# Weight blocks split into two parts by transfers instead of by engines, in a three-layer transformer kernel

## The chip, the cores and the metric

The kernel runs on one core of one Trainium2 chip. The metric is the device time of one execution in microseconds (us). The engines that appear below are PE (TensorE, matrix products; PEld is its weight load), DVE (VectorE), ACT (ScalarE), POOL (GpSimd) and SP (SyncE, which here does nothing but issue transfers). Each has its own queue and works through it in order.

## The reference, cut to what matters

The model has three layers on 512 tokens of 1024 features, all in float32: a mixer (forgetting attention and chunked attention) and a squared-relu MLP, a second mixer (stick-breaking and latent attention) and a second such MLP, and a third, hybrid mixer with a SwiGLU. Almost all of its time goes into products with weight matrices:

```python
x = x + even_mixer(h, w_in_ab, ..., w_out_ab)
x = x + jnp.square(jax.nn.relu(rmsnorm(x, g) @ w_up)) @ w_down
x = x + odd_mixer(h, positions, w_in_cd, ..., w_out_cd)
...
h = h + (jax.nn.silu(u @ w_gate) * (u @ w_up)) @ w_down
```

## The kernel before, in words

Float32 products are made from two short numbers. Every operand is kept as a rounded part (hi, type float32r) and the rest (lo), and a product W x is summed from three matmuls: hi hi, hi lo and lo hi. Activations are split where they arise. Weights are split where they are loaded.

The weights lie in DRAM as one flat array of blocks of 128 partitions by at most 1120 columns; most are 128x1024, 512 KB, which is eight stationary pieces of 128x128. `wblock` (line 584) brings one block: it loads the block into a raw tile (tag `wr`) with a transfer on SP's queue, ACT copies the raw tile into `wh`, which rounds it, and DVE subtracts `wh` from the raw tile into `wl`. There are two buffers of each of the three tags (`BUFS`, line 543). `gemm` (line 594), `gemm_iter` and `gemm_tok` call `wblock` and issue 24 matmuls of 512 columns to a full block: per piece two with `wh` and one with `wl`. In the last down projection some blocks go to tiles of tag `h`.

The order of the instructions is made on the host. The program is first recorded (`Recorder.add`, line 286), with the tiles that each instruction reads and writes. `Recorder.schedule` (line 390) then runs a list schedule: it keeps a clock for each engine, takes the ready instruction of lowest priority number, and hands out a tag's buffers in a fixed turn. The order that comes out for each engine is the order of its queue on the chip. Its costs are in `cost` (line 321) and `LAT` (line 355): a transfer takes 450 ns of its issuing engine when the source is DRAM, then 650 ns, then its bytes at 360 per ns, one transfer after the other; what waits for it starts 910 to 950 ns later if SP issued it, and 70 to 135 ns later if POOL issued it. In the kernel before, POOL issues no transfer at all. POOL's queue holds sums of squares (`acc`), the product of the SwiGLU's gate with a norm row (`T<-T,rbc`), softmax scaling, masks and the small `rsqrt` of the norms.

The program's stretches in time: first mixer 0 to 262 us, first MLP to 618, second mixer to 922, second MLP to 1278, third mixer to 1718 (its last 118 us are output projections with no attention beside them), SwiGLU and final norm to the end. Nearly every instruction carries line 371 in the profile, since one line issues all that was recorded; so the rows are told apart by the names of the tiles.

Of the kernel before, what the change touches and what calls it, by code (L numbers as in the profile page):

```python
# [11 lines left out]
F32 = mybir.dt.float32  # L12
# [6 lines left out]
T = 512  # L19
# [16 lines left out]
# --------------------------------------------------------------------------  # L36
# host side: layouts only
# --------------------------------------------------------------------------
class Packer:
    """Weights as one flat array of contiguous [128, width] blocks."""  # L40
# [12 lines left out]
    def stationary(self, key, w, cols=None):  # L53
        """[128 K, 128 M] pieces in the order (m, kt), eight to a block."""
        if cols is not None:
            w = w[:, cols]
        k, m = w.shape
        kt, nm = k // 128, m // 128
        sub = w.reshape(kt, 128, nm, 128).transpose(2, 0, 1, 3).reshape(nm * kt, 128, 128)
        blocks = [  # L60
            np.ascontiguousarray(sub[s:s + 8].transpose(1, 0, 2)).reshape(128, -1)
            for s in range(0, nm * kt, 8)
        ]
        self._add(key, blocks, (kt, nm))

    def moving(self, key, w, cols=None):
        """[128 K, N] pieces, as many k tiles to a block as WB columns hold."""
        if cols is not None:
            w = w[:, cols]
        k, n = w.shape  # L70
        kt = k // 128
        sub = w.reshape(kt, 128, n)
        blocks = [
            np.ascontiguousarray(sub[s:s + WB // n].transpose(1, 0, 2)).reshape(128, -1)
            for s in range(0, kt, WB // n)
        ]
        self._add(key, blocks, (kt, n))
# [8 lines left out]
class Columns:  # L86
    """Small [128, n] arrays side by side."""
# [137 lines left out]
# --------------------------------------------------------------------------  # L225
# order of the instructions: what the program does is recorded first, then
# issued engine by engine in the order of a list schedule
# --------------------------------------------------------------------------
# [20 lines left out]
class Recorder:  # L249
# [13 lines left out]
    @contextmanager  # L263
    def later(self, k):
        """what is recorded inside yields to the next k instructions, but for those that wait for it"""
        old, self.shift = self.shift, k
        yield
        self.shift = old

    def flush(self):  # L270
        """all that is recorded so far comes first"""
        for op in self.ops:
            op.prio = min(op.prio, len(self.ops))
# [80 lines left out]
    # from the end of one instruction to the start of a dependent one on another engine  # L354
# [26 lines left out]
    def sequence(self):  # L381
        """the instructions by priority: each before those that wait for it, what comes later in its own order"""
        first = math.inf
        for op in reversed(self.ops):
            op.prio = min([op.prio] + [self.ops[k].prio for k in op.succ])
            if op.group:
                op.prio = first = min(op.prio, first)
        return sorted(self.ops, key=lambda o: (o.prio, o.n))
# [110 lines left out]
# --------------------------------------------------------------------------  # L499
# chip side  # L500
# --------------------------------------------------------------------------
class Net:
# [21 lines left out]
    def fetch(self, m, tag="x"):  # L524
        """residual tile m on chip"""
        if self.x[m] is None:
            self.x[m] = self.tl(tag, [128, 512])
            self.nc.sync.dma_start(self.x[m], self.xd[m])
        return self.x[m]
# [13 lines left out]
    BUFS = {"x": 8, "T": 3, "G": 3, "P": 3, "wr": 2, "wh": 2, "wl": 2, "V": 8, "o": 6, "KK": 4, "QS": 2, "AB": 2, "h": 8, "X4": 4,  # L543
# [29 lines left out]
    def split(self, dst, src, scale=None):  # L573
        """dst[:, 0] + dst[:, 1] = src (* scale per partition), two short parts."""
        nc = self.nc
        hi, lo = dst[:, 0], dst[:, 1]
        if scale is None:
            nc.scalar.activation(hi, src, AF.Copy)
            nc.vector.tensor_tensor(lo, src, hi.bitcast(F32), ALU.subtract)
        else:  # L580
            nc.scalar.activation(hi, src, AF.Copy, scale=scale)
            nc.vector.scalar_tensor_tensor(lo, src, scale, hi.bitcast(F32), ALU.mult, ALU.subtract)

    def wblock(self, key, b, tags=("wh", "wl")):
        nc = self.nc
        off, w = self.pk.index[key][0][b]
        raw = self.tl("wr", [128, WB])[:, :w]
        hi, lo = (self.tl(t, [128, WB if t[0] == "w" else 1024], F32R) for t in tags)
        nc.sync.dma_start(raw, self.ins["w"][off:off + 128 * w].rearrange("(p c) -> p c", p=128))
        nc.scalar.activation(hi[:, :w], raw, AF.Copy)  # L590
        nc.vector.tensor_tensor(lo[:, :w], raw, hi[:, :w].bitcast(F32), ALU.subtract)
        return hi, lo

    def gemm(self, key, mov, evac, tags="gggggggg", cols=slice(0, 512), kept=None):
        """out[m] = W[:, m]^T mov; evac(m, psum)."""
# [17 lines left out]
    def gemm_tok(self, key, stat, evac, blk=None):  # L613
        """out[token tile i] = stat^T W; evac(i, psum)."""
# [33 lines left out]
    def mean_cols(self, acc, n, eps=None):  # L648
        """[128 tokens, tiles] mean of squares (+ eps)."""
        nc = self.nc  # L650
        ps = self.psum("s")
        nt = acc.shape[1] // 128
        for i in range(nt):
            nc.tensor.matmul(ps[:, i:i + 1], acc[:, 128 * i:128 * i + 128], self.c("ones"), start=True, stop=True)
        ms = self.small(nt)
        if eps is None:
            nc.vector.tensor_scalar(ms, ps[:, :nt], 1.0 / n, None, ALU.mult)
        else:
            nc.vector.tensor_scalar(ms, ps[:, :nt], 1.0 / n, eps, ALU.mult, ALU.add)
        return ms  # L660
# [8 lines left out]
    def rows(self, col, outs):  # L669
        """[128, 512] with col[token] in every row; outs = [(tag, factor)]."""  # L670
# [12 lines left out]
    def prep(self, m, gain, spill=False, sq=0):  # L683
        """operand x*g of feature tile m and its share of the sum of squares."""
# [29 lines left out]
    def to_stack(self, ab):  # L714
        """per head [hi; lo]"""
# [8 lines left out]
    def to_dup(self, ab):  # L724
        """per head a tile (hi, lo) with its rows twice"""
# [18 lines left out]
    def softmax(self, i, passes, bias, gate=None):  # L744
        """P [128 q, keys] from negated scores, normalised."""
# [14 lines left out]
    def turn(self, ps_list):  # L760
        """four P tiles -> per key tile j [128 keys, (hi, lo), q]"""
# [19 lines left out]
    def fold(self, o, dst, u):  # L781
        """O = rows 0:64 + rows 64:128, into half u of dst"""
# [5 lines left out]
    def v_tiles(self, key, stat, rcol, extra=None, blk=None):  # L788
        """value tiles [128 tokens, 4 heads, (hi, lo), 64]"""
# [55 lines left out]
    def out_part(self, key, ops):  # L845
        """first part of an output projection, one residual tile at a time"""
# [14 lines left out]
    def even_mixer(self):  # L861
# [20 lines left out]
        # sums within a token tile, and of the tiles one, two and three before  # L882
# [196 lines left out]
    def sincos(self, pos, freq, tag="strip"):  # L1079
        """cos and sin of position * frequency (frequencies along partitions)"""  # L1080
# [10 lines left out]
        # n = nh + nl, both short enough for exact products with the parts of 2 pi  # L1091
# [24 lines left out]
    def rope(self, pa, pb, c, s, tag):  # L1116
        """(x1 c - x2 s, x2 c + x1 s), each split"""
# [56 lines left out]
    def prep2(self, m):  # L1174
        """x * final gain * mixer gain, sums of x^2 and of (x * final gain)^2"""
# [13 lines left out]
    def hybrid_mixer(self):  # L1189
# [19 lines left out]
        # for the residual of the second block  # L1209
        rx, = self.rows(r1, [("strip", 1.0)])  # L1210

        # lambda
# [13 lines left out]
        # differential attention  # L1226
# [30 lines left out]
        # keys, values and gates of the second branch  # L1257
# [71 lines left out]
        # gated output of the first branch  # L1329
# [86 lines left out]
    def gemm_iter(self, key, mov):  # L1416
        """like gemm, one output tile at a time"""
# [76 lines left out]
    def compress(self, n, src):  # L1494
        """silu(windows @ w1), hidden units along partitions: [128, 2, (group, 32 windows)]"""
# [34 lines left out]
    def cmp_tiles(self, hk, hv, late):  # L1530
# [5 lines left out]
        # values: the windows of a group four times along the partitions  # L1536
# [12 lines left out]
        # keys: [hi; hi], [lo; lo] over (group, window)  # L1549
# [3 lines left out]
        # the windows of a group between zeros, so that a slice puts them at any of four places  # L1553
# [213 lines left out]
```

## Time and profile before

| | |
|---|---|
| time, median of 3 runs | 2093.58 us (2093.03 to 2095.36) |
| span of the profiled execution | 2093.9 us |
| PE busy | 2038.8 us, 97% |
| DVE, ACT, POOL busy | 1131.0, 896.5, 399.1 us |
| transfers on SP's queue | 230.25 MB, 35.9% of 16 DMA engines |

The page names busy time by engine, the busy share in slices, the transfer queues, the chain of work that ended last, and the costliest groups of instructions. A group's name is output<-inputs by tile names. Idle time before an instruction is put down to what released it. Times are us unless marked ns.

### The profile page before, as it was taken

Reading aid. Unit: us, or ns where it says so; the run is one execution under the profiler, and the core shown is the slowest. Engines: PE = TensorE matmul, PEld = TensorE weight load, DVE = VectorE, ACT = ScalarE, POOL = GpSimd, SP = SyncE. Lnnn points to the kernel's source line nnn. Section 1 sums busy time; section 2 is a strip of 40 time slices with the busy share of each in tenths; the row PEclk is TensorE's granted clock in tenths of the full one; section 3 lists DMA queues with packets and bytes.
Section 4 is the critical chain, followed back from the end, with each engine's and each line's share of the span. In section 5 each row is a group of like instructions: output and inputs, shape, how many; then the busy total and the mean of one; then the engine's idle time right before and its main releaser. Section 6 shows DMA issues by size and latency. Waiting matters only on the chain. (4 is left out here: it accounts for less than half of the span.)

```text
span 2093.9 us, 27228 instructions
## 1 busy us (share of the span) xinstructions
PE 2038.8 (97%) x9958; PEld 1688.3 (81%) x9958; DVE 1131.0 (54%) x2033; ACT 896.5 (43%) x1621; POOL 399.1 (19%) x524
## 2 busy tenths in 40 slices
PE   8999999999999999899999999989999999999998
PEld 7887878888888877778888888877788888888887
DVE  5657853443445666774434344766786644333334
ACT  5556542322335555643323243544685542222224
POOL 2343210000022453220000014212240221011013
PEclk9999999999999999999999999999999999999999
DMA  6445623323244415632333234474113222223222
GB/s 197 133 129 157 186 91 92 100 91 101 91 142 122 111 58 129 181 104 91 100 92 98 94 120 131 126 185 126 57 41 111 92 100 91 101 91 101 90 101 81
DMA packets 80294, 232.00 MB, mean 111 GB/s; under 512 B 11424, under 2 KB 15392, under 8 KB 80160
## 3 DMA queue, kind: packets, MB, share of 16 engines
q1 hardware_dynamic: 80160, 230.25, 35.9%
q8 instruction: 79, 1.29, 0.3%
q14 instruction: 55, 0.45, 0.1%
HBM read 183.04 MB, written 10.49 MB: 92 GB/s over the span
## 5 line engine op out<-in xcount | busy, mean ns | idle before, releaser
L371 PE MATMUL psg<-h,wh 128*128 128x512 f32 x2688 | 855.4, 396 | 0.9 <-ACT h L371 0.6
L371 ACT ACTIVATE wh<-wr 128x1024 fp32r<-128x1024 f32 (+3 forms) x313 | 326.6, 1043 | 864.3 <-PE psg L371 687.4
L371 PEld LDWEIGHTS psg<-h,wh 128*128 128x128 f32 x2688 | 504.3, 189 | 108.2 <-ACT h L371 1.4
L371 PE MATMUL psg<-h,wl 128*128 128x512 f32 x1344 | 532.5, 396 | 1.0 <-DVE wl L371 0.7
L371 DVE TENSOR_TENSOR wl<-wr,wh 128x1024 fp32r<-128x1024 f32 (+3 forms) x313 | 385.0, 1230 | 58.8 <-ACT wh L371 54.8
L371 PEld LDWEIGHTS psg<-h,wl 128*128 128x128 f32 x1344 | 253.9, 189 | 56.6 <-DVE wl L371 2.7
L371 PE MATMUL psg<-KK,wh 128*128 128x512 f32 (+1 forms) x788 | 240.6, 387 | 0.4 <-DVE V L371 0.2
L371 DVE TENSOR_TENSOR x<-psg,x 128x512 f32<-128x512 f32 (+1 forms) x120 | 78.2, 654 | 290.8 <-PE psg L371 290.7
L371 POOL TENSOR_TENSOR acc<-acc,T 128x512 f32<-128x512 f32 (+1 forms) x50 | 73.5, 1471 | 789.6 <-issue 639.5
L371 PE MATMUL psg<-V,wh 128*128 128x512 f32 (+1 forms) x672 | 207.9, 390 | 1.0 <-DVE G L371 1.0
L371 PEld LDWEIGHTS psg<-KK,wh 128*128 128x128 f32 x788 | 146.6, 188 | 32.2 <-ACT o L371 0.5
L371 PE MATMUL psg<-KK,wl 128*128 128x512 f32 (+1 forms) x394 | 151.7, 385 | 0.0
L371 PEld LDWEIGHTS psg<-V,wh 128*128 128x128 f32 x672 | 126.2, 189 | 29.0 <-ACT wh L371 1.1
L371 DVE SCALAR_TENSOR_TENSOR T<-psg,rbc 128x512 f32<-128x512 f32 x64 | 44.3, 692 | 174.9 <-PE psg L371 172.6
L371 PE MATMUL psg<-V,wl 128*128 128x512 f32 (+1 forms) x336 | 131.6, 392 | 0.0
L371 ACT ACTIVATE x<-x,sm 128x128 f32<-128x128 f32 (+1 forms) x192 | 106.6, 558 | 52.5 <-DVE sm L371 52.0
L371 PE MATMUL psg<-o,wh 128*128 128x512 f32 x384 | 127.7, 401 | 0.8 <-ACT wh L371 0.5
L371 PE MATMUL psg<-wh,h 128*128 128x256 f32 (+2 forms) x560 | 114.2, 291 | 6.7 <-ACT wh L371 6.7
L371 PE MATMUL pso<-pt,V 128*128 128x128 f32 (+3 forms) x432 | 108.0, 337 | 3.5 <-ACT pt L371 1.9
L371 POOL TENSOR_SCALAR x<-x,sm 128x128 f32<-128x128 f32 (+1 forms) x112 | 66.5, 599 | 173.2 <-DVE sm L371 121.0
L371 PEld LDWEIGHTS psg<-wh,h 128*128 128x128 f32 x560 | 92.0, 193 | 8.4 <-ACT wh L371 6.7
L371 POOL TENSOR_TENSOR T<-T,rbc 128x512 f32<-128x512 f32 x22 | 39.3, 1785 | 285.3 <-ACT T L371 285.3
(263 smaller groups left out, 2673.8 us busy)
## 6 DMA issues: line engine op xcount, KB each, us to landing
wr<-in_w_dram SPq DMA_DIRECT2D x302, 512.0 KB, 3.5
KK<-AB SPq DMA_DIRECT2D x48, 256.0 KB, 5.4
QS<-AB SPq DMA_DIRECT2D x48, 128.0 KB, 3.9
x<-xs SPq DMA_DIRECT2D x24, 256.0 KB, 3.3
xs<-P SPq DMA_DIRECT2D x16, 256.0 KB, 3.8
xs<-x SPq DMA_DIRECT2D x16, 256.0 KB, 2.0
h<-AB SPq DMA_DIRECT2D x16, 256.0 KB, 3.8
KK<-AB SPq DMA_DIRECT2D x32, 128.0 KB, 2.4
```

Source lines behind the costliest of these rows:

```text
L371: op.inst = getattr(getattr(nc, op.eng), op.name)(*op.args, **op.kw)
```

## The change

`wblock` no longer has a raw tile. A transfer issued by POOL (`nc.gpsimd.dma_start`) reads the float32 block from DRAM and casts it into the float32r tile `wh`. ACT writes the negated `wh` into `wl`. A second transfer issued by POOL reads the same block from DRAM again and adds it onto `wl` (`accum_op=ALU.add`), which leaves block minus `wh`. DVE's subtraction is gone. `wh` and `wl` have three buffers each instead of two; tag `wr` is no longer used. The diff also takes out comments and docstrings, which is left out here.

```diff
-    BUFS = {"x": 8, "T": 3, "G": 3, "P": 3, "wr": 2, "wh": 2, "wl": 2, "V": 8, ...
+    BUFS = {"x": 8, "T": 3, "G": 3, "P": 3, "wr": 2, "wh": 3, "wl": 3, "V": 8, ...
...
     def wblock(self, key, b, tags=("wh", "wl")):
         nc = self.nc
         off, w = self.pk.index[key][0][b]
-        raw = self.tl("wr", [128, WB])[:, :w]
         hi, lo = (self.tl(t, [128, WB if t[0] == "w" else 1024], F32R) for t in tags)
-        nc.sync.dma_start(raw, self.ins["w"][off:off + 128 * w].rearrange("(p c) -> p c", p=128))
-        nc.scalar.activation(hi[:, :w], raw, AF.Copy)
-        nc.vector.tensor_tensor(lo[:, :w], raw, hi[:, :w].bitcast(F32), ALU.subtract)
+        src = self.ins["w"][off:off + 128 * w].rearrange("(p c) -> p c", p=128)
+        nc.gpsimd.dma_start(hi[:, :w], src)
+        nc.scalar.activation(lo[:, :w], hi[:, :w].bitcast(F32), AF.Copy, scale=-1.0)
+        nc.gpsimd.dma_start(lo[:, :w], src, accum_op=ALU.add)
         return hi, lo
```

## Rows read from the trace of the kernel before

**Rows 1.** The page, part 1: busy us, share of the span, instructions.
```profile
span 2093.9 us, 27228 instructions
PE 2038.8 (97%) x9958; PEld 1688.3 (81%) x9958; DVE 1131.0 (54%) x2033; ACT 896.5 (43%) x1621; POOL 399.1 (19%) x524
```
**Rows 2.** Busy by stretch: us, engines busy (x), PEclk, DMA share, GB/s.
```profile
0.00:262.00 262.00, 250.13 (x1428) 214.18 (x1429) 178.59 (x413) 148.05 (x323) 87.82 (x157) 1.00 0.55 160
262.00:618.00 356.00, 353.88 (x1531) 288.90 (x1530) 154.68 (x176) 118.28 (x150) 14.24 (x9) 0.99 0.31 99
618.00:922.00 304.00, 284.12 (x1525) 238.04 (x1524) 207.10 (x401) 169.62 (x362) 110.78 (x184) 0.99 0.43 122
1278.00:1718.00 440.00, 429.06 (x2208) 351.64 (x2208) 292.41 (x691) 230.84 (x489) 109.64 (x120) 0.99 0.35 106
```
**Rows 3.** Instructions on tile wr by stretch: us, DVE busy (x), ACT busy (x).
```profile
262.00:618.00 356.00, 77.73 (x64) 67.95 (x64) 0.99 0.31 99
1600.00:1718.00 118.00, 27.91 (x22) 23.30 (x22) 1.00 0.27 95
```
**Rows 4.** The chain that ended last, in order of time: start us, us, what.
```profile
1721.74 345.57 PE psg L371 x1582
```
**Rows 5.** Timeline of ACT in the SwiGLU: start us, us, instruction, [idle before <-releaser].
```profile
1754.52 1.06 ACT L371 ACTIVATE wh<-wr 128x1024 fp32r<-128x1024 f32 x1 [3.97 <-PE psg L371]
1755.48 0.61 ACT L371 ACTIVATE T<-T 128x512 f32<-128x512 f32 x1
...
1765.56 1.06 ACT L371 ACTIVATE wh<-wr 128x1024 fp32r<-128x1024 f32 x1 [3.97 <-PE psg L371]
```
**Rows 6.** Waits, whole kernel: engine, for what: us in total, times, longest us.
```profile
ACT wh L371 <- PE psg L371: 687.4, 204, 5.2
...
PE psg L371 <- ACT wh L371: 7.2, 2, 6.7
...
PE psg L371 <- DVE wl L371: 2.0, 4, 1.0
...
SPq L371 <- DVE wl L371: 1347.4, 270, 27.4
```
**Rows 7.** Costliest groups: the subtraction: xcount | busy us, mean ns | idle before.
```profile
L371 DVE TENSOR_TENSOR wl<-wr,wh 128x1024 fp32r<-128x1024 f32 (+3 forms) x313 | 385.0, 1230 | 58.8 <-ACT wh L371 54.8
```
**Rows 8.** Tile wr, 1722 to 2045: ns min/median/max, first and last start; landing us.
```profile
L371 SPq DMA_DIRECT2D wr<-in_w_dram x59: 327/328/328, 1723.3 to 2044.1; - x59
L371 ACT ACTIVATE wh<-wr x58: 1061/1064/1067, 1726.8 to 2041.7; 128x1024 fp32r<-128x1024 f32 x58
...
  ACT wh L371: 10.1, 40
...
DMA to landing us min/median/max: 3.1/3.2/3.8
```
**Rows 9.** Busy in that stretch, with DMA share and GB/s.
```profile
1722.00:2045.00 323.00, 323.00 (x1405) 264.04 (x1405) 125.58 (x139) 86.86 (x103) 39.07 (x22) 1.00 0.28 95
```
**Rows 10.** POOL by group: xcount | busy us, mean ns | idle before.
```profile
L371 POOL TENSOR_TENSOR T<-T,rbc 128x512 f32<-128x512 f32 x22 | 39.3, 1785 | 285.3 <-ACT T L371 285.3
...
L371 POOL TENSOR_TENSOR sm<-sm,cst 128x4 f32<-128x4 f32 (+1 forms) x15 | 14.7, 979 | 59.0 <-DVE sm L371 59.0
```
**Rows 11.** Tile wr, whole kernel: the issues and the landing.
```profile
L371 SPq DMA_DIRECT2D wr<-in_w_dram x317: 327/328/2131, 1.7 to 2056.1; - x159
...
DMA to landing us min/median/max: 2.0/3.5/8.4
```
**Rows 12.** Busy before and after the second MLP's norm.
```profile
915.00:920.00 5.00, 4.00 (x17) 2.74 (x15) 4.43 (x6) 4.87 (x7) 2.82 (x3) 1.00 0.39 108
920.00:925.00 5.00, 4.28 (x15) 3.70 (x16) 1.23 (x2) 2.56 (x4) 1.69 (x2) 0.62 0.29 101
```
**Rows 13.** Timeline of PE there.
```profile
918.50 0.50 PE L371 MATMUL psg<-h,wh 128*128 128x512 f32 x1
920.72 1.45 PE L371 MATMUL pss<-cst,acc 128*128 128x1 f32 x8 [1.72 <-POOL acc L371]
922.03 0.77 PE L371 MATMUL psg<-h,wh 128*128 128x512 f32 x1
```

More of the change, by code (lines that the diff above doesn't have):

```diff
@@ L541, in c @@
         return self.ct[:, o:o + n]
-    BUFS = {"x": 8, "T": 3, "G": 3, "P": 3, "wr": 2, "wh": 2, "wl": 2, "V": 8, "o": 6, "KK": 4, "QS": 2, "AB": 2, "h": 8, "X4": 4,
+    BUFS = {"x": 8, "T": 3, "G": 3, "P": 3, "wr": 2, "wh": 3, "wl": 3, "V": 8, "o": 6, "KK": 4, "QS": 2, "AB": 2, "h": 8, "X4": 4,
             "sm": 16, "sm32": 3, "rbc": 1, "rbcq": 1, "strip": 2}
```

## The prediction

> **What bounds the kernel now.** I read the busy times first, then stretches, then one block in the steady part, then who waits for weights. PE is busy 2038.8 us of a span of 2093.9 us, so 55 us is all that is not PE [rows 1]. In the first MLP it is busy 353.88 of 356 us [rows 2], and the chain that ended last is one unbroken run of 1582 matmuls, 345.57 us, in the SwiGLU [rows 4]. There a block comes round every 5.5 us: the ACT copies of the rows shown lie 1765.56 - 1754.52 = 11.04 us apart with one between them [rows 5], and 59 block loads were issued in 320.8 us, 320.8/58 = 5.53 us [rows 8]. That is PE's own pace for 24 matmuls. The reader is to see in the waits that the weights come early: ACT waits 687.4 us in all for PE to free a `wh` buffer, while PE waits 7.2 us for `wh` and 2.0 us for `wl`; SP's queue waits 1347.4 us to be allowed to load the next raw block [rows 6]. So the work of splitting is hidden today, and what the change takes away from DVE is worth almost nothing by itself. What it puts in its place must stay under 5.53 us a block.
>
> **Blocks at full pace and others.** The first MLP has 64 blocks [rows 3]; the other MLP stretches show the same 64 each, and the output projections at the end of the third mixer 22 [rows 3]. That is 214 blocks at 5.53 us. Of 317 loads [rows 11] 103 remain, in mixer stretches of 262 + 304 + (440 - 118) = 888 us, 8.6 us apart. POOL is busy 87.82 + 110.78 + 109.64 = 308 us in the three mixers [rows 2], about 2.4 us a block for their 126 blocks.
>
> **Removed.** 313 subtractions, 385.0 us of DVE [rows 7]. They lie beside PE; DVE is at 54% [rows 1]. Worth 0 to the 2.0 us that PE waits for `wl` [rows 6]. SP loses 317 issues of 0.33 us [rows 11] and its 1347 us of waiting for raw buffers, so that the operand moves queued behind them go out sooner. PE's gaps bound that gain at 55 us in all; I take 5 us. ACT's pass stays, one per block at 1.06 us [rows 8], now after the transfer instead of before PE's release: no difference in busy time.
>
> **Added: two POOL issues per block.** POOL issued no transfer, so no row shows the price. Ends: 0.33 us, SP's issue of the same transfer [rows 8], and 1.79 us, POOL's costliest group [rows 10]. I take 0.98 us, its 128x4 operation [rows 10]: a POOL instruction with almost no data, which is nearest to one that only prepares a transfer. 634 of them are 621 us on top of 399 [rows 1], so POOL is not full; order is what matters.
>
> **Added: the casting transfer.** It moves the bytes of today's load. Ends 3.1 us from issue to landing, the least in the SwiGLU [rows 8], and 8.4 us, the most anywhere [rows 11]. I take the median 3.2 us of the undisturbed stretch [rows 8]. On the engines a block takes 0.28 x 5.53 = 1.55 us [rows 9].
>
> **Added: the accumulating transfer.** It reads the block from DRAM again and must also read what lies in `wl`. Ends: 1.55 us of the DMA engines, if the addition costs nothing, and 8.4 us by the slowest landing [rows 11]. I take two loads' worth, 3.1 us, because twice the bytes are read. The Trainium skill, page "Collectives: The Full Stack", section "The bandwidth ceiling: the fold count and why AG ≠ RS ≠ AR", says that a summing transfer needs two source reads on one ring and that copying is 1.93 times as fast; no run here shows that. As an estimate from that page the transfer would be 1.55 x 1.93 = 3.0 us and the total below about 25 us lower.
>
> **Added: a wait in POOL's queue.** The accumulating issue waits for ACT, which waits for the cast's landing. Queued behind it on POOL are the next block's cast and whatever sums, masks and softmax scalings the plan put there; PE and DVE wait for those, and ACT's evacuations queue behind the negation. The plan's own figures put the accumulating issue 0.45 + 0.65 + 1.46 + 0.075 + 0.95 + 0.17 = 3.75 us after the cast's issue (costs in the code), and the next cast when PE frees a buffer, one block later. So POOL's order is cast, accumulate, cast, accumulate, and one round of it is a chain: cast lands 3.2, hand-off to ACT and back 2 x 0.25 (10.1 us of waits over 40 copies [rows 8]) with ACT 1.06 between, accumulate issued. If the next cast is queued right behind it, its data come after the accumulating transfer's on the same DMA engines. The issue time drops out, because transfers move while the next is prepared: round = 3.2 + 0.5 + 1.06 + accumulating transfer = 4.76 + 3.1 = 7.9 us. With an addition that costs nothing it is 4.76 + 1.55 = 6.3 us; with nothing in front of the cast and SP's price of issue 4.76 + 0.33 = 5.1 us, under PE's 5.53.
>
> **The sum.** At 7.9 us the 214 full-pace blocks cost 214 x (7.9 - 5.53) = 507 us. In the mixers a round of 7.9 us fits into 8.6 us if POOL's other 2.4 us fall into the waits, and overruns by 1.7 us if they don't; I take half, 103 x 0.85 = 88 us. Minus 5 us. The third buffer does not help against a round that repeats for every block; it covers latency only: two blocks' time, 11.06 us, from release to need. Total 2094 + 507 + 88 - 5 = 2684 us, against the profiled span of 2093.9 us, which is the median of the runs to 0.02%. I say **2680 us**. With the ends of the terms: additions that cost nothing 2094 + 214 x 0.77 + 0 - 5 = 2254 us; a cast that lands only after 8.4 us, round 13.1 us, 2094 + 214 x 7.53 + 103 x 4.5 - 5 = 4164 us.
>
> **The rivals.** *Nothing to see* (0.10): casts find free buffers early and run ahead, round 5.1 us, PE stays the bound: 2085 to 2120 us. For it: 4.76 us leaves 0.8 us of slack. Against: the plan lets a cast go only when PE has released a buffer, and the accumulating transfer is due half a microsecond before. *Faster* (0.06): the same, and three buffers with SP's queue emptied close PE's gaps in the mixers, where 55 us lie less the start and the final norm; it decides below a round of 5.53 us, and gives 2075 us. *Half hidden* (0.17): addition at the price of a copy, round 6.0 to 6.5: 2190 to 2300 us. *PE loses its clock* (0.22): each late block leaves PE idle. At the second MLP's norm PE stood still for 1.72 us, had only eight one-column matmuls, and the granted clock went from 1.00 to 0.62 [rows 12, 13], that is, from 2.4 GHz to mostly 1.2 GHz; a 512-column matmul then took 0.77 us in place of 0.50 [rows 13]. At half the clock a block takes up to 2 x 5.53 = 11.1 us: 2094 + 214 x 5.53 + 103 x 2.5 = 3535 us. It decides where the idle time per block is near that gap; at 7.9 us it is 2.4 us, and matmuls of full width stand on both sides, so I give it the smaller chance. The Trainium skill, page "TensorE: Matmul & The Clock Gate", section "What's actually happening", holds the low clock to be the default that only activity lifts; by that rule, too, a starved PE is slowed twice; the rows agree. *The change does something else*: if the cast kept all bits, `wl` would be zero, with the same transfers and time; that moves no number here.
>
> **How the numbers follow.** Forecast (round 6.5 to 9 us, 2300 to 3000 us) 0.45; nothing to see 0.10; faster 0.06; half hidden 0.17; lost clock or transfers slower than I took 0.22. A measurement of this kernel can tell about 0.2% from no change, 4 us. Faster by more than that: 0.06 and 0.01 of nothing to see, 0.07. Within it 0.05. Slower 0.88. The range leaves out faster and part of nothing to see below, and the far part of the last case above: 2110 to 3550 us.
>
> **What would show it.** Right: in the MLPs POOL's accumulating issue waits for ACT, ACT's negation waits for the landing of the cast, and PE waits for the transfer into `wl`, over 2 us a block; the blocks come every 7 to 9 us; the DMA share rises above 0.5. Wrong in size: the pace of the blocks, from which the two landing times can be read apart. Wrong in kind: PE still 97% busy, or PE waiting in the mixers only, or the granted clock well below 1.

## The result and the profile after

The changed kernel takes 2839.94 us (2837.65 to 2851.07, median of 4 runs) against 2094.47 us (2093.03 to 2100.32) of the kernel before beside it. The ratio is 1.357, with a 95% interval of 1.354 to 1.360: slower by 745 us. The forecast was 2680 us, slower, in a range of 2110 to 3550 us. The profiled execution has a span of 2837.5 us, 743.6 us more than that of before.

Busy time first, to be held against [rows 1]: engine, us, share of the span, instructions.

```profile
span 2837.5 us, 27499 instructions
PE 2296.1 (81%) x9958; PEld 1809.7 (64%) x9958; DVE 769.2 (27%) x1716; ACT 896.5 (32%) x1621; POOL 805.7 (28%) x1158
```

PE fell from 97% to 81%, and no other engine took its place: DVE lost its 362 us net, POOL gained 407 us for 634 transfers and is still idle for 72% of the span. Where no engine is busy all the time, a chain of waits is the likely limit. To see where, the span is cut at the norms' `rsqrt` on POOL, which lie in both kernels at the start of an MLP and at its end. Before (the stretches with an MLP or the SwiGLU, then the mixers), then after; us, busy us of PE, PEld, DVE, ACT and POOL (instructions), granted clock, share of the DMA engines, GB/s.

```profile
272.15:628.11 355.96, 355.95 (x1563) 291.68 (x1562) 149.99 (x170) 118.45 (x150) 13.61 (x8) 0.99 0.32 101
922.45:1279.26 356.81, 356.62 (x1544) 291.11 (x1544) 150.72 (x175) 121.67 (x155) 21.77 (x16) 0.99 0.32 101
1719.61:2093.90 374.29, 364.14 (x1727) 303.71 (x1725) 147.32 (x178) 108.05 (x144) 55.73 (x41) 0.99 0.27 93
```
```profile
0.00:272.15 272.15, 258.16 (x1460) 220.41 (x1461) 188.56 (x424) 151.60 (x329) 92.04 (x159) 0.99 0.55 158
628.11:922.45 294.34, 274.47 (x1462) 229.48 (x1461) 201.97 (x395) 165.91 (x355) 107.18 (x182) 0.99 0.43 120
1279.26:1719.61 440.35, 429.50 (x2210) 351.92 (x2211) 292.41 (x691) 230.84 (x489) 108.77 (x119) 0.99 0.35 106
```

```profile
0.00:334.62 334.62, 277.73 (x1458) 231.85 (x1459) 149.17 (x390) 157.74 (x333) 132.35 (x229) 0.93 0.76 180
334.62:864.70 530.08, 415.81 (x1562) 316.61 (x1560) 72.60 (x106) 114.43 (x146) 101.49 (x137) 0.91 0.58 131
864.70:1228.51 363.81, 300.85 (x1464) 247.13 (x1464) 165.71 (x359) 166.70 (x355) 151.05 (x256) 0.90 0.63 141
1228.51:1754.86 526.35, 416.83 (x1559) 318.27 (x1560) 74.61 (x112) 121.02 (x155) 110.08 (x144) 0.91 0.59 133
1754.86:2298.56 543.70, 466.75 (x2199) 368.78 (x2198) 236.29 (x636) 230.22 (x489) 176.46 (x228) 0.93 0.60 138
2298.56:2837.50 538.94, 418.17 (x1719) 327.06 (x1719) 70.86 (x114) 106.40 (x143) 134.30 (x168) 0.91 0.56 128
```

The three stretches with an MLP or the SwiGLU grew by 530.1 - 356.0, 526.4 - 356.8 and 538.9 - 374.3 us, 508 us in all. The mixers were 272.2, 294.3 and 440.4 us; they grew by 62.5, 69.5 and 103.3 us, 235 us in all. Together that is the 743.6 us. A block of the first MLP (64 of them) takes 530.1/64 = 8.28 us in place of 356.0/64 = 5.56 us.

The waits of the whole kernel after, against [rows 6]: engine, for what: us in total, times, longest.

```profile
POOL wl L371 <- ACT wl L371: 1529.5, 273, 13.0
ACT wl L371 <- DMA wh<-in_w_dram: 1202.8, 223, 12.8
...
PEld psg L371 <- DMA wl<-in_w_dram: 498.9, 220, 6.3
PE psg L371 <- DMA wl<-in_w_dram: 407.0, 212, 5.9
...
POOL wh L371 <- PE psg L371: 137.6, 64, 9.8
```

POOL waits for ACT, ACT for the cast's landing, PE for the accumulating transfer. POOL waits 137.6 us for PE to free a buffer, where ACT waited 687.4 us for that before: over the whole kernel, free buffers are not what is short. One round in the SwiGLU, from the timelines of POOL, then ACT, then PE (start us, us, instruction, [idle before <-releaser]):

```profile
2443.33 0.85 POOL L371 DMA_DIRECT2D wl<-in_w_dram  x1 [6.51 <-ACT wl L371]
2443.88 0.87 POOL L371 DMA_DIRECT2D wh<-in_w_dram  x1
2451.42 0.85 POOL L371 DMA_DIRECT2D wl<-in_w_dram  x1 [6.67 <-ACT wl L371]
```
```profile
2450.06 1.06 ACT L371 ACTIVATE wl<-wh 128x1024 fp32r<-128x1024 f32 x1 [7.03 <-DMA wh<-in_w_dram]
```
```profile
2440.63 0.50 PE L371 MATMUL psg<-KK,wl 128*128 128x512 f32 x1 [2.05 <-DMA wl<-in_w_dram]
...
2448.80 0.50 PE L371 MATMUL psg<-KK,wl 128*128 128x512 f32 x1 [2.35 <-DMA wl<-in_w_dram]
```

The cast is issued 0.55 us after the accumulating transfer of the block before; ACT starts 6.18 us later, runs 1.06 us, and 0.30 us on the next accumulating transfer goes out: 0.55 + 6.18 + 1.06 + 0.30 = 8.09 us, and PE gets its block every 8.17 us. The landings in the first MLP, 380 to 840 us (first `wh`, then `wl`; min, median, max us from issue):

```profile
DMA to landing us min/median/max: 5.9/6.2/6.8
```
```profile
DMA to landing us min/median/max: 5.2/5.5/5.8
```

The cast, a transfer of 512 KB like the one that took 3.2 us in [rows 8], lands after 6.2 us: it was queued right behind the accumulating one, and the experiments below show what that costs.

### The profile page after: what moved, and what is told of

Read it like the earlier page. It is cut to its first block, busy times and chain, and to the rows that moved or that the text cites. A ratio compares the mean times of both kernels' runs of the same rounds, so it can differ in the third digit from the quotient of the medians.

```text
span 2837.5 us, 27499 instructions
## 1 busy us (share of the span) xinstructions
PE 2296.1 (81%) x9958; PEld 1809.7 (64%) x9958; DVE 769.2 (27%) x1716; ACT 896.5 (32%) x1621; POOL 805.7 (28%) x1158
## 4 chain that ended last, share of the span: by engine, by line
issue 55%; PE 16%; POOL 16%; DMA 9%; ACT 2%; DVE 1%; SPq 0%; POOLq 0%; DVEq 0%; ACTq 0%
PE psg L371 9%; POOL wh L371 6%; POOL wl L371 5%; DMA wh<-in_w_dram 4%; DMA wl<-in_w_dram 3%; PE pss L371 3%; PE psp L371 2%; PE pso L371 2%; POOL T L371 1%; POOL acc L371 1%; ACT wl L371 1%; POOL x L371 1%; DMA x<-in_x_dram 1%; POOL G L371 0%; DVE x L371 0%
## 5 line engine op out<-in xcount | busy, mean ns | idle before, releaser
L371 PE MATMUL psg<-h,wh 128*128 128x512 f32 x2688 | 917.6, 421 | 0.0
L371 ACT ACTIVATE wl<-wh 128x1024 fp32r<-128x1024 f32 (+3 forms) x313 | 325.4, 1040 | 1564.8 <-DMA wh<-in_w_dram 1202.8
L371 PE MATMUL psg<-h,wl 128*128 128x512 f32 x1344 | 580.1, 432 | 198.2 <-DMA wl<-in_w_dram 198.1
L371 POOL DMA_DIRECT2D wl<-in_w_dram x313 | 272.6, 873 | 1637.9 <-ACT wl L371 1529.5
L371 PEld LDWEIGHTS psg<-h,wh 128*128 128x128 f32 x2688 | 545.9, 204 | 122.2 <-issue 2.3
L371 POOL DMA_DIRECT2D wh<-in_w_dram x313 | 244.8, 782 | 149.4 <-PE psg L371 137.6
L371 PE MATMUL psg<-KK,wh 128*128 128x512 f32 (+1 forms) x788 | 279.9, 441 | 1.2 <-DVE G L371 0.7
L371 PEld LDWEIGHTS psg<-KK,wl 128*128 128x128 f32 x394 | 87.7, 223 | 219.9 <-DMA wl<-in_w_dram 203.1
L371 PE MATMUL psp<-cst,x 128*128 128x128 f32 x440 | 89.7, 289 | 21.8 <-POOL x L371 13.8
L371 PE MATMUL psg<-o,wl 128*128 128x512 f32 x192 | 82.8, 435 | 28.2 <-DMA wl<-in_w_dram 28.2
```

Source lines behind the costliest of these rows:

```text
L371: op.inst = getattr(getattr(nc, op.eng), op.name)(*op.args, **op.kw)
```

## The experiments

The first five test the theory that the round is a chain of cast, negation and addition whose transfers share one queue. What is compared in each is the length of the first MLP, 64 blocks, from norm to norm; the kernel before, run beside them, took 2095.8 to 2098.6 us. Each time of an experiment is one run.

**The addition's price.** The second transfer casts the block over `wl` instead of adding to it.

```diff
-        nc.gpsimd.dma_start(lo[:, :w], src, accum_op=ALU.add)
+        nc.gpsimd.dma_start(lo[:, :w], src)
```

> The second transfer overwrites wl with a cast of the block instead of adding onto it, so wl holds the wrong numbers; order, waits and buffers stay as in the changed kernel. Theory (a round of POOL's queue sets the pace: the cast's data stand behind the accumulating transfer's on the DMA engines, then landing, ACT, next issue): only the accumulating transfer's 3.1 us shrinks to 1.55 us, the round from 8.1 to about 6.5 us, 2094 + 214 x 0.95 + some 50 us in the mixers = about 2350 us. Rival (the transfers' fixed latency and POOL's issue set the pace, not the bytes that the addition reads): 8.1 us a block stay, 2800 to 2840 us.

Measured: 2415.7 us; the first MLP 419.5 us, 6.55 us a block. Its stretch, and the landings of `wh` and of `wl` in it:

```profile
316.79:736.31 419.52, 374.04 (x1561) 287.15 (x1559) 72.61 (x106) 114.77 (x146) 78.25 (x136) 1.00 0.52 166
```
```profile
DMA to landing us min/median/max: 4.4/4.6/5.0
```
```profile
DMA to landing us min/median/max: 3.7/3.8/4.3
```

Without the addition the second transfer lands 1.7 us sooner (3.8 against 5.5), the cast queued behind it 1.6 us sooner (4.6 against 6.2), and the round is 1.73 us shorter. So the addition alone costs 424 us of the 745. The rest is there with two casts. The pace is the expected one, the total 66 us above it.

**No second transfer.** `wl` stays the negated `wh`.

```diff
-        nc.gpsimd.dma_start(lo[:, :w], src, accum_op=ALU.add)
```

> The second transfer is left out: wl stays the negated wh, which is wrong for lo; the cast on POOL's queue and ACT's negation stay. Theory (the chain through POOL's queue needs the second issue): nothing on POOL waits for ACT any more, casts go as soon as PE releases a buffer, three buffers cover 3.2 + 0.9 + 1.3 us; PE is the bound again, 2085 to 2110 us. Rival (a cast issued by POOL is slow by itself, or POOL's queue delays it behind softmax work): the mixers stay 100 to 235 us longer, 2200 to 2350 us.

Measured: 2160.4 us, between the two expectations. In the first MLP a block takes 360.0/64 = 5.62 us and PE is busy throughout:

```profile
295.26:655.21 359.95, 359.95 (x1573) 293.66 (x1573) 72.75 (x106) 118.92 (x146) 44.27 (x73) 1.00 0.35 100
```

One cast per block is hidden there; its landing is 3.8 us. What is left of the 65 us lies mostly in the mixers (295.3, 304.4 and 460.0 us: 23 + 10 + 20 us more than before). The three kernels give the engines' time of each transfer in the same stretch, DMA share times pace: 0.35 x 5.62 = 1.97 us a block with the cast alone, 0.52 x 6.55 = 3.41 with a second cast behind it, 0.58 x 8.28 = 4.80 with the accumulating one. By these shares a second cast adds 1.44 us, an accumulating transfer 2.83 us, 1.97 times as much. Each of the two without the other, over the whole kernel (this run, and the addition alone further below; q0 is the queue of POOL's transfers: packets, MB, share of the 16 engines' span), gives a smaller factor:

```profile
q0 software_dynamic: 45648, 162.81, 26.5%
```
```profile
q0 software_dynamic: 45648, 162.81, 36.2%
```

That is 0.265 x 2158.7 = 572 us for the casts and 0.362 x 2626.1 = 951 us for the same bytes added, 1.66 times as much. The Trainium skill ("Collectives: The Full Stack", "The bandwidth ceiling: the fold count and why AG ≠ RS ≠ AR") has copying 1.93 times as fast as summing, measured between the ranks of a ring; the 1.66 to 1.97 of these runs lie around that.

**Two buffers.** The third buffer of each tag is undone, the rest is the changed kernel.

```diff
-    ... "wr": 2, "wh": 3, "wl": 3, ...
+    ... "wr": 2, "wh": 2, "wl": 2, ...
```

> The third buffers of wh and wl are undone, all else as in the changed kernel. Theory (the round in POOL's queue sets the pace, and buffers don't): with two buffers a block is ready 0.2 + 4.1 + 1.3 + 5.4 = 11 us after PE released the one two before, so two blocks take 11 + 5.5 us, 8.2 us each, the same pace by another limit; 2840 to 2950 us. Rival (the latency of the whole way from release to wl is the limit already with three buffers, about 8.1 x 3 - 5.5 = 19 us): two buffers give (19 + 5.5)/2 = 12 us a block, about 3900 us.

Measured: 3201.2 us, 595.0/64 = 9.30 us a block, between the two. From POOL's timeline:

```profile
599.31 0.87 POOL L371 DMA_DIRECT2D wl<-in_w_dram  x1 [6.70 <-ACT wl L371]
603.64 0.55 POOL L371 DMA_DIRECT2D wh<-in_w_dram  x1 [3.46 <-PE psg L371]
610.21 0.86 POOL L371 DMA_DIRECT2D wl<-in_w_dram  x1 [6.01 <-issue]
610.76 0.87 POOL L371 DMA_DIRECT2D wh<-in_w_dram  x1
```

Every other cast now waits for PE, too. So the third buffer is worth 1.0 us a block, 361 us of the whole: it does hide latency, and the forecast that it "does not help against a round that repeats" holds only for the part of the round that is left.

Because the casts wait for PE here, they follow the accumulating transfer at different distances, and this shows whether the time between the two issues matters. In the SwiGLU, POOL, and the landing of the cast of 2714.42:

```profile
2712.23 0.89 POOL L371 DMA_DIRECT2D wl<-in_w_dram  x1 [2.10 <-ACT wl L371]
2714.42 0.56 POOL L371 DMA_DIRECT2D wh<-in_w_dram  x1 [1.30 <-PE psg L371]
```
```profile
DMA to landing us min/median/max: 4.5/4.5/4.5
```

Issued 2.19 us after the accumulating transfer, this cast lands 2.19 + 4.5 = 6.7 us after that one's issue. Over the whole run the median of this time is 6.9, 7.0, 6.9 and 6.7 us for casts issued 0.5 to 1, 1 to 1.5, 1.5 to 2 and 2 to 2.5 us behind (41, 38, 37 and 11 of them). In the changed kernel, where the distance is 0.55 us, it is 0.55 + 6.2 = 6.75 us. Within 2.5 us a cast that is issued later does not land later: its landing is set by the accumulating transfer ahead of it and not by its own issue.

**The order in POOL's queue.** Nothing is changed but the order: where a cast follows an accumulating transfer in POOL's queue, it is put in front of it, so that the cast travels while ACT's result is awaited.

```diff
-            for op in (self.schedule() if reorder else ops):
+            order = self.schedule() if reorder else ops
...
+                if add(order[a]) and order[b].name == "dma_start" and not add(order[b]):
+                    after[b] = order[a]
...
+            for op in order:
```

> The changed kernel with one thing moved: wherever the next block's cast follows the accumulating transfer directly in POOL's queue, the cast goes first. Same transfers, bytes, buffers and order on all other engines. Theory (the order in POOL's queue makes the round a chain): the cast no longer stands behind the accumulating transfer, nor the next cast behind a wait for ACT; what is left is that a cast waits for PE's release and the accumulating transfer of the block before goes out after it: a block is ready 0.2 + 0.9 + 5.5 + 0.3 = 6.9 us after the release of the block two before, two blocks take 12.4 us, 6.2 us each: 2094 + 214 x 0.67 + 50 to 180 us in the mixers = 2290 to 2420 us. Rival (the addition's reading, or POOL's issuing, is the pace whatever the order): 8.1 us a block, 2800 us and more.

And the same end by another way: the plan is given costs as the trace shows them, an issue of 0.56 us, a longer latency, and twice the bytes for an addition, and finds its own order.

```diff
+        if op.name == "dma_start" and e == "gpsimd":
+            return 560
...
-                dma = max(dma, end + 650) + nbytes / 360
+                slow = 2 if "accum_op" in op.kw else 1
+                dma = max(dma, end + (1700 if e == "gpsimd" else 650)) + slow * nbytes / 338
```

> The changed kernel, with the plan's costs for POOL's transfers set to what the chip showed (0.56 us of POOL, 1.7 us of latency, an addition twice as long); the plan then puts the next cast ahead of the accumulating transfer for 173 of 313 blocks instead of 34, and in pairs. All engines' orders follow the new plan. Theory (order): two blocks share one round, about 12 us for two, 6.0 to 6.7 us each: 2250 to 2420 us. Rival (order is no matter): 2800 us and more.

Measured: 2609.0 us with the swap and 2449.9 us with the plan told; the first MLP takes 432.2 and 427.4 us, 6.75 and 6.68 us a block. The swap falls between its two expectations, the told plan just outside its own in the total and at the end of it in the pace. POOL's timeline in the swapped kernel, its main wait in the first MLP, and the landings of `wh` and of `wl` there:

```profile
501.49 0.54 POOL L371 DMA_DIRECT2D wh<-in_w_dram  x1 [7.61 <-PE psg L371]
502.01 0.91 POOL L371 DMA_DIRECT2D wl<-in_w_dram  x1
507.03 0.54 POOL L371 DMA_DIRECT2D wh<-in_w_dram  x1 [4.10 <-PE psg L371]
507.56 0.91 POOL L371 DMA_DIRECT2D wl<-in_w_dram  x1
```
```profile
POOL wh L371 <- PE psg L371: 310.5, 63, 8.5
```
```profile
DMA to landing us min/median/max: 3.8/4.5/5.5
```
```profile
DMA to landing us min/median/max: 5.3/6.8/8.8
```

The same transfers, the same bytes and the same buffers, and 1.5 us a block less with POOL's order alone changed (1.6 us with the plan told): the order that the plan chose was a cause by itself. POOL now waits for PE to free a buffer, as ACT did in [rows 6]; the cast lands after 4.5 us. But the addition is now queued behind the cast and lands after 6.8 us (5.5 before), and PE still waits for `wl`. The swap alone does not reach the mixers (337.6 us in the first, 562.3 in the third) and leaves the SwiGLU at 488.5 us, which is more than 6.75 us a block would give; why was not looked into. The plan told is better there (451.7 us); it changed the order on all engines, the swap on POOL alone.

**The cast alone.** The raw tile is loaded by SP as before and DVE subtracts; only `wh` comes by POOL's casting transfer. First with two buffers of each tag, then with one raw tile, three `wh` and two `wl`.

```diff
+        raw = self.tl("wr", [128, WB])[:, :w]
         nc.gpsimd.dma_start(hi[:, :w], src)
-        nc.scalar.activation(lo[:, :w], hi[:, :w].bitcast(F32), AF.Copy, scale=-1.0)
-        nc.gpsimd.dma_start(lo[:, :w], src, accum_op=ALU.add)
+        nc.sync.dma_start(raw, src)
+        nc.vector.tensor_tensor(lo[:, :w], raw, hi[:, :w].bitcast(F32), ALU.subtract)
```

> Only the cast is taken from the change: wh by the casting POOL transfer, the raw block by SP into wr as before, wl by DVE's subtraction; two buffers of each as before, ACT's pass gone. Theory (the casting transfer alone is no burden): a block is ready 0.2 + 4.1 + 0.25 + 1.23 + 0.25 = 6.0 us after the release, two blocks take 11.5 us, 5.8 us each against 5.53: 2110 to 2180 us. Rival (software transfers land as late as in the changed kernel, 6.1 us): 8.0 us after the release, 6.8 us each, 2094 + 214 x 1.25 + mixers = about 2400 us.

> The cast alone, as in the run with DVE's subtraction kept, with the buffers dealt out anew: one raw, three of wh, two of wl. Theory (the 5.9 us a block of that run come from two buffers of wh against 4.5 us of landing): the cast runs one block further ahead, the MLPs go back to 5.5 us a block, and only the mixers keep the 30 to 55 us each that POOL's queue costs them: 2190 to 2240 us. Rival (software transfers slow the MLPs by themselves): 2280 us and more.

Measured: 2300.5 us and 2204.2 us; the first MLP takes 5.89 and 5.68 us a block. With three `wh` buffers the cast is all but hidden where the blocks come evenly. What remains lies in the mixers (300.0, 320.0 and 471.8 us: 28 + 26 + 31 us more than before) and the SwiGLU (16 us). The expected total of the first missed for the same reason: its mixers cost 36, 36 and 58 us.

**The addition alone.** SP loads the raw tile, ACT rounds it into `wh`, DVE negates `wh` into `wl`, and only the addition is POOL's; two buffers of each.

```diff
-        nc.gpsimd.dma_start(hi[:, :w], src)
-        nc.scalar.activation(lo[:, :w], hi[:, :w].bitcast(F32), AF.Copy, scale=-1.0)
+        nc.sync.dma_start(raw, src)
+        nc.scalar.activation(hi[:, :w], raw, AF.Copy)
+        nc.vector.tensor_scalar(lo[:, :w], hi[:, :w].bitcast(F32), -1.0, None, ALU.mult)
         nc.gpsimd.dma_start(lo[:, :w], src, accum_op=ALU.add)
```

> Only the accumulating transfer is taken from the change: raw by SP and wh by ACT as before, wl first the negated wh by DVE, then the block added by POOL; two buffers of each. Theory: no chain over two blocks in POOL's queue, but the way from PE's release to wl is 0.2 + 1.06 + 0.25 + 0.7 + 0.2 + 5.5 + 0.2 = 8.1 us, two blocks take 13.6 us, 6.8 us each: 2094 + 214 x 1.3 + 0 to 100 us = 2370 to 2480 us. Rival (an accumulating transfer is as slow as 8.1 us a block by itself): 2800 us and more.

Measured: 2627.8 us, 452.5/64 = 7.07 us a block, and an addition that lands after 6.0 us although no cast stands in its queue. It cannot start until PE has freed the block and ACT and DVE have been through, so its whole landing lies between release and need. The total missed the expectation, as in the runs before, by the mixers (the first is 90 us longer than before).

**What the mixers pay for.** The theory by then was that transfers and POOL's softmax work hold each other up in one queue. Nearly all of that work is given to DVE (22 lines of this kind), in the changed kernel, in the kernel with the cast alone (1, 3, 2 buffers), and, as a control, in the kernel before.

```diff
-        nc.gpsimd.tensor_scalar(p[:, :n], p[:, :n], m[:, 2:3], 1.0 if gate is None else gate(i), ALU.mult, ALU.mult)
+        nc.vector.tensor_scalar(p[:, :n], p[:, :n], m[:, 2:3], 1.0 if gate is None else gate(i), ALU.mult, ALU.mult)
```

> The changed kernel with nearly all of POOL's other work (sums, softmax scalings, products, memsets; not the triangular masks and not the norms' pow) given to DVE, which is at 27%. Question: why the mixers cost 235 us more than before. Theory (POOL's queue is in order, so a transfer waits behind a softmax scaling that itself waits for DVE, and the scaling behind a transfer's wait): the mixers' surcharge falls from 62.5 + 69.5 + 103.4 us to 60 to 110 us in all, of which some 59 us are the 22 blocks at full pace in the third mixer; the MLPs stay at 8.28 us a block; total 2665 to 2715 us. Rival (the round of the two transfers itself is too long for the mixers, whatever stands beside it): mixers change by less than 25 us, total 2810 to 2850 us.

> The cast alone by POOL with buffers wr 1, wh 3, wl 2 (2204 us, mixers +28, +26, +30 us, SwiGLU +16 us) and POOL's other work given to DVE in the same way. Theory (neighbours in the queue): the mixers' surcharge falls from 84 us to 0 to 30 us; total 2110 to 2150 us. Rival (the cast comes too late by itself): total above 2185 us. If it comes out under 2085 us, the cast alone would beat the kernel before.

> Control: the kernel before with the same work moved from POOL to DVE. DVE goes from 54% to some 65% busy. Expected by both: within 25 us of 2094 us, so that what the other two show is the transfers' queue and not the move.

Measured: 2840.0, 2224.4 and 2116.1 us. The mixers of the changed kernel with its POOL relieved, by stretch:

```profile
0.00:331.58 331.58, 275.75 (x1468) 228.81 (x1468) 179.67 (x512) 157.35 (x331) 62.38 (x108) 0.96 0.77 182
858.80:1218.22 359.42, 298.96 (x1469) 247.43 (x1470) 189.66 (x474) 165.05 (x355) 77.10 (x141) 0.90 0.65 143
1743.19:2304.85 561.66, 467.96 (x2197) 368.07 (x2197) 269.19 (x749) 230.09 (x489) 82.93 (x115) 0.92 0.58 133
```

They are 59, 65 and 121 us longer than before, 246 us where it was 235. POOL lost 308 us of work, and the time moved by nothing. The control's mixers are 28 us longer than those of the kernel before, so the move itself has a price, and with that taken off the relief is worth at most 17 us. The theory falls: POOL's other work is not what the mixers pay for. The rival's number came true, but that the round itself is the price is argued below, not shown. Nor does relieving POOL help the cast alone (20 us slower, as much as the control's 19).

That the round costs so much in stretches where blocks come 8.6 us apart on average is seen in how they come. ACT's copies in the second mixer of the kernel before:

```profile
641.88 1.06 ACT L371 ACTIVATE wh<-wr 128x1024 fp32r<-128x1024 f32 x1 [4.67 <-PE psg L371]
647.52 1.06 ACT L371 ACTIVATE wh<-wr 128x1024 fp32r<-128x1024 f32 x1 [4.04 <-issue]
652.98 1.06 ACT L371 ACTIVATE wh<-wr 128x1024 fp32r<-128x1024 f32 x1 [3.88 <-issue]
660.81 1.05 ACT L371 ACTIVATE wh<-wr 128x1024 fp32r<-128x1024 f32 x1
```

They come 5.6, 5.5 and 7.8 us apart, in a burst; the longest gap in this mixer is 31 us. Of the 122 gaps in the three mixers 83 are shorter than 8.2 us. If each of these were stretched to 8.2 us and no long gap gave anything back, the mixers would be 248 us longer. Measured were 235 us. This is a reckoning after the fact, not an experiment of its own, and it agrees in the sum better than mixer by mixer (48, 87 and 113 us against 62.5, 69.5 and 103.3). Done with the paces of other runs it comes near for the second cast (6.55 us: 121 us, measured 133), and falls short for two buffers (9.3 us: 346, measured 429), for the addition alone (7.07 us: 158, measured 267) and for the swap (6.75 us: 134, measured 253). So the pace of the MLPs explains a part of what the mixers pay, and not all.

Of the 235 us, 83 are PE's own busy time, which rose from 962 to 1045 us in the mixers at a granted clock of 0.90 to 0.93 (0.99 before); 152 are time in which it stood still. POOL's waits in the second mixer of the changed kernel show that free buffers are short there, other than in the MLPs:

```profile
POOL wl L371 <- ACT wl L371: 73.2, 21, 13.0
...
POOL wh L371 <- PE psg L371: 51.0, 20, 9.6
```

**What stays open.** How the mixers' 235 us divide between the round, the wait for free buffers, PE's clock and the operand moves, which land later among the added transfers (`x<-xs` after 5.9 us, 3.3 before), no run separates. Why the cast alone costs the mixers 85 us, with `wh` three deep, is not settled; the raw tile gave the kernel before a place to hold blocks ahead of PE that a cast straight into `wh` does not have, but no run separates that. A fourth buffer wasn't tried. No version found beats the kernel before; PE is busy for all but 55 us there.

## Why the prediction came out as it did

*Kind and sign.* Right. The order on POOL (cast, accumulate, in step), ACT waiting for the cast's landing and PE for `wl`, and a DMA share above 0.5 (0.56 to 0.59 in the MLP stretches) are what the traces show. PE waits 112.2 us for `wl` over the 64 blocks of the first MLP, 1.8 us a block where over 2 us was said; PE's matmuls at a lower clock fill the rest, see below.

*The round, forecast 7.9 us, measured 8.1 in the steady part and 8.28 over the stretch.* From the accumulating transfer's issue to the cast's landing 3.2 + 3.1 = 6.3 us was forecast, 0.55 + 6.2 = 6.75 us was measured. That "the issue time drops out" held: with two buffers, casts issued 0.5 to 2.5 us behind the accumulating transfer landed 6.7 to 7.0 us after its issue all the same. The term that was too small is the cast's 3.2 us, taken from SP's load: issued by POOL with nothing queued ahead, the cast lands after 3.8 us (the run with no second transfer). The addition's 3.1 us of the DMA engines was near (2.83 by shares, 3.0 for the addition alone: 951 us over 317 blocks). The hand-off after ACT was 0.3 us where 0.5 was taken for both ways together, so two errors partly cancel, and that 7.9 came so near 8.1 is partly luck. The further 0.2 us of the whole stretch were not followed up. With 8.28 us the 192 blocks of the MLPs give 508 us where 192 x 2.37 = 455 us was forecast, 53 us too little; the 22 blocks of the output projections add some 7 us.

*The mixers, forecast 88 us.* The step that failed most. Without the 22 full-pace blocks (22 x 2.7 = 59 us) the other 103 cost 235 - 59 = 176 us, 1.7 us each and not 0.85. The "half" was a guess between two ends about POOL's other work, and the run without that work shows that at most 17 us hang on it. The mean spacing of 8.6 us was the wrong row to read, as far as the gaps above tell; what makes up the rest of the 176 us stays open. (The mixers have 103 + 22 = 125 blocks, not 126; nothing hangs on it.)

*The gain of 5 us* from the freed SP queue: nothing of it can be seen. 53 + 7 + 88 + 5 = 153 us is what the sum lacked against the span.

*Issue price, 0.98 us taken between 0.33 and 1.79.* Measured 0.53 us for a cast, 0.85 us for an accumulating one and for a cast right behind it. POOL's busy time was rightly put off the path.

*The rivals.* "Half hidden" (round 6.0 to 6.5 us, 2190 to 2300 us) is the kernel with the second cast: 6.55 us, but 2416 us, since the mixers cost more there, too. "Nothing to see" came true of the first MLP with the cast alone, three `wh` deep (5.68 us a block), and not of its total of 2204 us. *PE loses its clock*: the granted clock did fall, to a mean of 0.91 in the MLPs, which is 2.4 GHz with stretches at 1.2 GHz in it, and PE's busy time in the first MLP rose from 356 to 416 us for the same matmuls. But POOL waits for PE there for only 0.9 us in all:

```profile
POOL wl L371 <- ACT wl L371: 405.0, 61, 7.6
...
PE psg L371 <- DMA wl<-in_w_dram: 112.2, 61, 3.4
...
POOL wh L371 <- PE psg L371: 0.9, 1, 0.9
```

So in the MLPs the slower matmuls fill time in which PE would have stood still; they do not lengthen the round. The Trainium skill ("TensorE: Matmul & The Clock Gate", "What's actually happening") holds the low clock to be the default that activity lifts; these rows agree. In the MLPs the low clock cost next to nothing; whether it cost something in the mixers, where POOL does wait for PE, no run shows.

## What to carry to other kernels

Work that an engine did beside the bottleneck was free here, and the transfers that replaced it were not, because their steps form a chain through one in-order queue. Write down one round of such a chain, with landing times of the kind of transfer that will be in it, and compare it with the pace of the bottleneck. Before transfers that depend on each other go into one queue, look which of them travels while the other's input is made: POOL's order alone was worth 231 us here, and 390 us with all engines planned anew for it. Where blocks come in bursts, look at the gaps between them and not at their mean alone.

## What was not expected of the hardware

- A transfer issued by POOL that casts 512 KB lands after 3.8 us with nothing queued ahead, little more than SP's 3.5 us in the kernel before [rows 11]; right behind an accumulating one it takes 6.2 us, behind another cast 4.6 us.
- The issue of an accumulating transfer takes POOL 0.85 to 0.91 us, that of a casting one 0.53 us; a cast issued right behind the accumulating one takes 0.87 us. These spans overlap: the cast's issue starts 0.55 us after that of the accumulating one.
- A cast issued 0.5 to 2.5 us behind an accumulating transfer lands 6.7 to 7.0 us after that one's issue, whenever it was issued itself (medians of the run with two buffers).
- Adding to `wl` in SBUF costs the DMA engines 1.66 to 1.97 times as much as a cast of the same block: 951 against 572 us when each is alone, 2.83 against 1.44 us a block as the second transfer.
- A cast that travels ahead delays the addition in turn: 6.8 us in place of 5.5 us in the swapped order.
